# Who makes the second half swap of the rotation: GpSimd in place of ScalarE

## The chip, the cores and the metric

The kernel runs on one core of a Trainium2 chip. A core has five engines that work side by side, each through its own instructions in program order: TensorE (PE, matmuls; PEld is its weight load), VectorE (DVE), ScalarE (ACT), GpSimd (POOL) and SyncE (SP, which here only issues DMAs). They wait for each other through semaphores. The metric is the device time of one execution in microseconds (us), smaller is better.

## What is computed

Two layers of a decoder trunk on 512 tokens of width 1024, in float32. Each layer is a norm, one input projection whose columns feed three token mixers (a state space group, a short convolution group, a sparse attention group), an output projection, and a gated MLP. The change lies in the attention group, where queries and keys are rotated by position:

```python
def apply_rope(x, cos, sin):
    x1, x2 = jnp.split(x, 2, axis=-1)
    ...
    return jnp.concatenate([x1 * c - x2 * s, x2 * c + x1 * s], axis=-1)

q = apply_rope(q.reshape(bsz, s_len, NSA_HEADS, dk), cos, sin) * (dk ** -0.5)
kc = compress_block(rope_k(k_cmp), kpos, kw1, kw2)
...
ks_blocks = rope_k(k_sel).reshape(bsz, n_slc, SEL_BLOCK, dk)
...
kw = jnp.pad(rope_k(k_win), win_pad)
```

A head has 64 channels, so a half is 32. The compressed keys kc and values vc come from a small MLP over blocks of 32 tokens, with a position table added first.

## The kernel before

Activations lie with channels on the 128 partitions and the 512 tokens along the free dimension. A projection tile is 128 output channels: 24 matmuls of 128x512 (`mul3` in `tile_steps`, L260 to L262: eight input blocks, three products of high and low parts) into one PSUM tile `mm`. Each weight tile is loaded by SyncE into `raw` and split into a high part by ScalarE (L227, or L219 for the MLP's weights) and a low part, either by VectorE (L224, L233) or by ScalarE's negated copy (L230, L221) and an accumulating DMA that GpSimd issues (L231, L222). Three `raw` and four `hl` buffers rotate. L262 is the first matmul of three that reads the low part.

Four tiles are rotated in each layer: `cmp` (64 rows rotated, 64 rows of values), `keys`, `q0` and `q1` (128 rows, so two heads of 64). For each, `evac` copies PSUM into a slot `r` (L331, ScalarE), then makes a second slot `sw` with the halves of each head swapped: for every 64 rows one copy of 32 rows up and one of 32 rows down (L333, L334). `rope` (L338 to L340, VectorE) multiplies `r` in place by the cosines, `sw` by the sines, and adds. So there are seven pairs of copies in a layer. The tables `Cr` and `Sr` already hold the norm's factor (L471, L472), which comes through `rstdB` (L316, ScalarE).

After the rope the keys are split into high and low parts on both halves of the partitions (L352, L353 on ScalarE, L354, L355 on VectorE) and the queries too (L396, L397). The rotated `cmp` tile gets its position table added by GpSimd (L373, two adds for each of four parts, with a memset L374 behind), is split (L379 ScalarE, L380 VectorE) and goes into the compress matmuls (L542, eight for each of four parts; their result is copied by L548). The scores are L673 and L676 on TensorE (high and low part of the keys), evacuated by VectorE (L678); probabilities come from ScalarE's exp (L680) and are scaled by VectorE and GpSimd (L687). Then come transposes (L697), their evacuation (L701, L704) and the product with the values (L717). L419 and L420 split the values, L407 to L409 evacuate the projection of small columns.

In which order each engine gets its instructions is set in two steps. The program issues pieces by a table (PLAN: when a piece comes, counted in projection steps). The Tile framework then orders the instructions of all engines by its own planned times and sets the semaphores; an engine afterwards keeps to that order. An edit that makes one instruction look shorter or longer to it, or moves it to another engine, can therefore move others.

Of the kernel before, what the change touches and what calls it, by code (L numbers as in the profile page):

```python
# [12 lines left out]
AF = mybir.ActivationFunctionType  # L13
# [52 lines left out]
def trunk(ctx: ExitStack, tc: tile.TileContext, ins, out):  # L66
    nc = tc.nc
    V, A, G, TE = nc.vector, nc.scalar, nc.gpsimd, nc.tensor
# [7 lines left out]
    def slot(dt=F32, shape=(P, 512)):  # L76
        return ph.tile(list(shape), dt, tag="s", bufs=32, name="s")
# [245 lines left out]
    def mixers(l, norm):  # L323
# [4 lines left out]
        def evac(ps, n):  # L328

            r, sw = slot(), slot()  # L330
            A.activation(r, ps, AF.Copy)  # L331
            for q in range(0, n, 64):
                A.activation(sw[q:q + 32], r[q + 32:q + 64], AF.Copy)  # L333
                A.activation(sw[q + 32:q + 64], r[q:q + 32], AF.Copy)  # L334
            return r, sw

        def rope(r, sw, n):
# [160 lines left out]
        def tile_steps(name, post, rot_n=0):  # L498
            wt = nxt()
            ps = mm()  # L500
            for k in range(KD):
                mul3(ps, wt, k, hs[k][:, 0, :], hs[k][:, 1, :], k == 0, k == KD - 1)
                step()
                if k < KD - 1:
                    yield
            args = evac(ps, rot_n) if rot_n else (ps,)
            if clock[0] < t_spread:
                late.append(lambda: post(*args))
            else:
                post(*args)  # L510
            done[name] = True
            yield
# [470 lines left out]
        r = PLAN["ratio"]  # L983
# [332 lines left out]
```

## Time and profile before

| what | value |
|---|---|
| time of the runs, median of 3 | 1210.34 us (1210.14 to 1210.81) |
| the profiled execution | 1209.18 us, span of the trace 1207.4 us |
| TensorE busy | 1177.0 us, 97% of the span |
| VectorE busy | 931.6 us, 77% |
| ScalarE busy | 664.0 us, 55% |
| GpSimd busy | 170.4 us, 14% |
| the rotated tiles are worked on | about 25 to 62 us (layer 0) and 618 to 652 us (layer 1) |

Busy times are sums over one profiled execution. A row of a time line gives start, duration, engine, line, operation, output and input tile with their shapes and, in square brackets, how long the engine had been idle and what ended that. Matmuls overlap in their rows (a matmul of 128x512 has a row of 0.39 us, and the next one starts 0.23 us later), so distances between starts are read, not durations. Where several instructions of one form follow each other, one row stands for them, with their number behind x.

### The profile page before, as it was taken

Reading aid. Unit: us, or ns where it says so; the run is one execution under the profiler, and the core shown is the slowest. Engines: PE = TensorE matmul, PEld = TensorE weight load, DVE = VectorE, ACT = ScalarE, POOL = GpSimd, SP = SyncE. Lnnn points to the kernel's source line nnn. Section 1 sums busy time; section 2 is a strip of 40 time slices with the busy share of each in tenths; the row PEclk is TensorE's granted clock in tenths of the full one; section 3 lists DMA queues with packets and bytes.
Section 4 is the critical chain, followed back from the end, with each engine's and each line's share of the span. In section 5 each row is a group of like instructions: output and inputs, shape, how many; then the busy total and the mean of one; then the engine's idle time right before and its main releaser. Section 6 shows DMA issues by size and latency. Waiting matters only on the chain.

```text
span 1207.4 us, 17074 instructions
## 1 busy us (share of the span) xinstructions
PE 1177.0 (97%) x6299; PEld 1001.1 (83%) x6299; DVE 931.6 (77%) x1707; ACT 664.0 (55%) x1060; POOL 170.4 (14%) x225
## 2 busy tenths in 40 slices
PE   8899999999999999999998999999999999999997
PEld 7677788888889888988887887888888998889886
DVE  5797879558888778967747887876787968888684
ACT  7885764444544445434569667545444544454464
POOL 2332245100000000000031212640000000000002
PEclk9999999999999999999999999999999999999999
DMA  7774554523225331443255834544232352325332
GB/s 261 180 174 106 122 149 118 153 87 102 91 62 149 122 101 60 129 135 111 81 116 146 189 98 134 158 109 135 88 105 70 106 157 88 105 61 152 119 123 88
DMA packets 46771, 146.07 MB, mean 121 GB/s; under 512 B 5024, under 2 KB 9440, under 8 KB 46688
## 3 DMA queue, kind: packets, MB, share of 16 engines
q1 hardware_dynamic: 36112, 117.71, 29.8%
q0 software_dynamic: 10432, 27.27, 12.7%
q8 instruction: 50, 0.82, 0.3%
q14 instruction: 33, 0.27, 0.1%
q10 hardware_dynamic: 144, 0.00, 0.0%
HBM read 115.57 MB, written 2.13 MB: 97 GB/s over the span
## 4 chain that ended last, share of the span: by engine, by line
PE 70%; DVE 16%; ACT 7%; issue 4%; POOL 1%; DMA 1%; SPq 0%; POOLq 0%; DVEq 0%; ACTq 0%
PE mm L260 16%; PE mm L262 16%; PE mm L261 16%; PE mm L1065 2%; PE mm L1063 2%; PE mm L1064 2%; PE aux L260 2%; PE aux L262 2%; PE aux L261 2%; PE aux L1065 2%; PE aux L1064 2%; PE aux L1063 2%; DVE hl L171 1%; DVE s L1011 1%; PE pv L717 1%
## 5 line engine op out<-in xcount | busy, mean ns | idle before, releaser
L260 PE MATMUL mm<-h,hl 128*128 128x512 f32 x1040 | 410.5, 395 | 0.0
L262 PE MATMUL mm<-h,hl 128*128 128x512 f32 x1040 | 407.3, 392 | 0.9 <-DMA hl<-raw 0.8
L261 PE MATMUL mm<-h,hl 128*128 128x512 f32 x1040 | 407.3, 392 | 0.0
L227 ACT ACTIVATE hl<-raw 128x1024 fp32r<-128x1024 f32 x161 | 170.2, 1057 | 149.1 <-PE mm L262 96.5
L262 PEld LDWEIGHTS mm<-h,hl 128*128 128x128 f32 x1040 | 195.8, 188 | 42.9 <-DMA hl<-raw 1.8
L260 PEld LDWEIGHTS mm<-h,hl 128*128 128x128 f32 x1040 | 195.9, 188 | 39.6 <-issue 0.7
L261 PEld LDWEIGHTS mm<-h,hl 128*128 128x128 f32 x1040 | 196.2, 189 | 38.7 <-issue 0.3
L233 DVE TENSOR_TENSOR hl<-raw,hl 128x1024 fp32r<-128x1024 f32 x119 | 146.2, 1229 | 48.0 <-ACT hl L227 47.2
L1011 DVE SCALAR_TENSOR_TENSOR s<-s,par 128x511 f32<-128x511 f32 (+1 forms) x172 | 128.0, 747 | 11.9 <-ACT s L1009 9.9
L1008 DVE TENSOR_TENSOR s<-mm,rstdB 128x512 f32<-128x512 f32 x86 | 59.0, 688 | 53.1 <-PE mm L262 53.1
L1009 ACT ACTIVATE s<-s,par 128x512 f32<-128x512 f32 x86 | 69.3, 807 | 28.7 <-DVE s L1008 28.1
L169 POOL DMA_DIRECT2D hl<-s x16 | 13.8, 863 | 496.1 <-DVE hl L171 441.7
L319 ACT ACTIVATE s<-s 128x512 fp32r<-128x512 f32 (+2 forms) x78 | 39.6, 524 | 62.5 <-DVE s L1026 57.8
L166 ACT ACTIVATE hl<-s 128x512 fp32r<-128x512 f32 x64 | 38.3, 629 | 54.4 <-PE aux L1065 24.9
L1024 ACT ACTIVATE s<-s 128x512 f32<-128x512 f32 x40 | 25.3, 631 | 57.4 <-DVE s L1011 57.4
L231 POOL DMA_DIRECT2D hl<-raw x42 | 36.5, 869 | 128.1 <-ACT hl L230 81.9
L1065 PE MATMUL mm<-s,hl 128*128 128x256 f32 x192 | 54.3, 283 | 0.0
L1063 PE MATMUL mm<-s,hl 128*128 128x256 f32 x192 | 54.3, 283 | 0.0
L1064 PE MATMUL mm<-s,hl 128*128 128x256 f32 x192 | 54.3, 283 | 0.0
L320 DVE TENSOR_TENSOR s<-s 128x512 fp32r<-128x512 f32 (+2 forms) x78 | 43.9, 578 | 8.9 <-ACT s L319 8.4
L274 POOL TENSOR_TENSOR m<-m,mhalf 128x1 f32<-128x1 f32 (+2 forms) x14 | 10.9, 776 | 259.4 <-DVE m L273 259.4
L230 ACT ACTIVATE hl<-raw 128x1024 fp32r<-128x1024 f32 x42 | 43.9, 1046 | 0.0
(299 smaller groups left out, 2329.9 us busy)
## 6 DMA issues: line engine op xcount, KB each, us to landing
raw<-in_w_up SPq DMA_DIRECT2D x86, 512.0 KB, 3.3
raw<-in_w_dn SPq DMA_DIRECT2D x49, 512.0 KB, 3.3
raw<-in_w_in SPq DMA_DIRECT2D x44, 512.0 KB, 3.7
hl<-raw POOLq DMA_DIRECT2D x44, 512.0 KB, 4.6
raw<-in_w_out SPq DMA_DIRECT2D x16, 512.0 KB, 3.3
raw<-in_w SPq DMA_DIRECT2D x8, 512.0 KB, 4.6
s<-dr SPq DMA_DIRECT2D x16, 256.0 KB, 4.7
hl<-s POOLq DMA_DIRECT2D x16, 256.0 KB, 3.6
```

The costliest lines, as they stand in the source:

```text
L227: A.activation(t[:, 0, 0:w], r[:, 0:w], AF.Copy)
L230: A.activation(t[:, 1, 0:w], r[:, 0:w], AF.Copy, scale=-1.0)
L233: eng.tensor_tensor(t[:, 1, 0:w], r[:, 0:w], t[:, 0, 0:w].bitcast(F32), op=OP.subtract)
L260: TE.matmul(ps, wh, rhs_h, start=first, stop=False)
L261: TE.matmul(ps, wh, rhs_l, start=False, stop=False)
L262: TE.matmul(ps, wl, rhs_h, start=False, stop=last)
L1008: V.tensor_tensor(u, ps, rstdB, op=OP.mult)
L1009: A.activation(acc, u, AF.Identity, scale=w[:, 2:3], bias=pr[:, C_FCB + i:C_FCB + i + 1])
L1011: V.scalar_tensor_tensor(acc[:, j:], u[:, :T - j], w[:, 2 - j:3 - j], acc[:, j:], op0=OP.mult, op1=OP.add)
L1063: TE.matmul(ps, w[:, 0, q], h_, start=first and j == 0, stop=False, skip_group_check=not first)
L1064: TE.matmul(ps, w[:, 0, q], l_, start=False, stop=False, skip_group_check=not first)
L1065: TE.matmul(ps, w[:, 1, q], h_, start=False, stop=j == 3, skip_group_check=not first)
```

## The change

In `evac` the second copy of each pair moves from ScalarE to GpSimd; the first stays.

```diff
             for q in range(0, n, 64):
                 A.activation(sw[q:q + 32], r[q + 32:q + 64], AF.Copy)
-                A.activation(sw[q + 32:q + 64], r[q:q + 32], AF.Copy)
+                G.tensor_copy(sw[q + 32:q + 64], r[q:q + 32])
```

GpSimd gets seven more instructions in each layer, 14 in all, and the order of the other engines changes with it. L338 now waits for GpSimd too, since it overwrites `r`, which the copies read. Four places follow, with the difference of an engine's order, - for before and + for now.

GpSimd, layer 0, from the position adds of the cmp tile on (s<-s,par_87 is a part of that tile with the position table added; the four pairs of L334 are two for keys, two for q0, two for q1):

```order
 L373 TENSOR_TENSOR s<-s,par_87 64x8x31 x4
 L374 MEMSET s 128x8
+L334 COPY s<-s 32x512 x2
 L373 TENSOR_TENSOR s<-s,par_87 64x8x31 x2
 L374 MEMSET s 128x8
 L373 TENSOR_TENSOR s<-s,par_87 64x8x31 x2
 L374 MEMSET s 128x8
-L231 DMA hl<-raw 128x1024 x3
+L334 COPY s<-s 32x512 x2
+L231 DMA hl<-raw 128x1024
+L334 COPY s<-s 32x512 x2
+L231 DMA hl<-raw 128x1024 x2
```

The two copies for the keys stand behind four of the eight adds, those for q0 and q1 behind all of them, and the first DMA L231 of this piece behind q0's copies.

TensorE, layer 0, in the tile behind q1 (h_81 and h_82 are input blocks 2 and 3; aux<-hl,s is the compress matmul):

```order
 L260 MATMUL mm<-h_81,hl 128x512
-L261 MATMUL mm<-h_81,hl 128x512
-L262 MATMUL mm<-h_81,hl 128x512
-L260 MATMUL mm<-h_82,hl 128x512
-L261 MATMUL mm<-h_82,hl 128x512
-L262 MATMUL mm<-h_82,hl 128x512
-L260 MATMUL mm<-h_83,hl 128x512
 L542 MATMUL aux<-hl,s 128x256 x7
 L542 MATMUL aux<-hl,s 64x256
+L261 MATMUL mm<-h_81,hl 128x512
+L262 MATMUL mm<-h_81,hl 128x512
+L260 MATMUL mm<-h_82,hl 128x512
```

The compress matmuls stand six projection matmuls earlier.

GpSimd, layer 1, the same stretch:

```order
 L373 TENSOR_TENSOR s<-s,par_88 64x8x31 x2
 L374 MEMSET s 128x8
-L231 DMA hl<-raw 128x1024 x3
+L231 DMA hl<-raw 128x1024
+L334 COPY s<-s 32x512 x4
+L231 DMA hl<-raw 128x1024
+L334 COPY s<-s 32x512 x2
+L231 DMA hl<-raw 128x1024
```

Here all eight adds and one DMA stand ahead of the copies of keys and q0.

VectorE, layer 1, the rope of the keys (hl<-raw,hl is a weight split):

```order
 L338 TENSOR_TENSOR s<-s,Cr 128x512
 L339 TENSOR_TENSOR s<-s,Sr 128x512
-L224 TENSOR_TENSOR hl<-raw,hl 128x8x128
 L340 TENSOR_TENSOR s<-s 128x512
-L224 TENSOR_TENSOR hl<-raw,hl 128x8x128
+L224 TENSOR_TENSOR hl<-raw,hl 128x8x128 x2
```

The weight split that stood inside the rope stands behind it. On TensorE of layer 1 the first score pairs (L673, L676) move ahead of the last six matmuls of a projection tile, as the compress matmuls do in layer 0. On ScalarE of layer 0 the two L419 move ahead of L316.

## Rows read from the trace of the kernel before

**Rows 1.** TensorE's waits, 20 to 100 us: us in total, times, longest.

```profile
...
PE aux L673 <- DVE s L397: 1.7, 1, 1.7
PE pv L717 <- DVE s L704: 0.5, 1, 0.5
PE mm L262 <- DMA hl<-raw: 0.5, 1, 0.5
```

**Rows 2.** Time line of TensorE, layer 0: start, duration, [idle before <-releaser].

```profile
46.73 1.21 PE L542 MATMUL aux<-hl,s 128*128 128x256 f32 x8 [2.04 <-DVE s L380]
...
48.25 0.60 PE L260 MATMUL mm<-h,hl 128*128 128x512 f32 x1
...
51.63 0.42 PE L262 MATMUL mm<-h,hl 128*128 128x512 f32 x1
...
56.47 0.39 PE L262 MATMUL mm<-h,hl 128*128 128x512 f32 x1
...
61.92 0.45 PE L673 MATMUL aux<-s 128*128 128x512 f32 x1
```

**Rows 3.** Time line of GpSimd, layer 0.

```profile
36.54 4.70 POOL L373 TENSOR_TENSOR s<-s,par 64x248 f32<-64x248 f32 x4 [1.49 <-DVE s L340]
...
51.49 0.86 POOL L231 DMA_DIRECT2D hl<-raw  x1 [6.11 <-DVE s L340]
```

**Rows 4.** Time line of VectorE, layer 0.

```profile
37.00 0.82 DVE L338 TENSOR_TENSOR s<-s,Cr 128x512 f32<-128x512 f32 x1 [0.55 <-ACT s L334]
...
40.57 1.22 DVE L340 TENSOR_TENSOR s<-s 128x512 f32<-128x512 f32 x1
...
46.25 0.76 DVE L380 TENSOR_TENSOR s<-s 128x256 fp32r<-128x256 f32 x2
```

**Rows 5.** Time line of ScalarE, layer 0.

```profile
41.82 0.63 ACT L352 ACTIVATE s<-s 64x512 fp32r<-64x512 f32 x1 [3.77 <-DVE s L340]
...
46.01 0.58 ACT L331 ACTIVATE s<-mm 128x512 f32<-128x512 f32 x1
...
50.16 1.04 ACT L230 ACTIVATE hl<-raw 128x1024 fp32r<-128x1024 f32 x1
```

**Rows 6.** Time line of GpSimd, layer 1.

```profile
623.31 3.42 POOL L373 TENSOR_TENSOR s<-s,par 64x248 f32<-64x248 f32 x4
...
630.84 0.87 POOL L231 DMA_DIRECT2D hl<-raw  x1 [0.41 <-issue]
```

**Rows 7.** Time line of VectorE, layer 1.

```profile
631.40 0.69 DVE L338 TENSOR_TENSOR s<-s,Cr 128x512 f32<-128x512 f32 x1 [3.40 <-ACT s L334]
...
633.74 0.69 DVE L340 TENSOR_TENSOR s<-s 128x512 f32<-128x512 f32 x1
...
638.01 0.76 DVE L380 TENSOR_TENSOR s<-s 128x256 fp32r<-128x256 f32 x2
640.90 0.69 DVE L338 TENSOR_TENSOR s<-s,Cr 128x512 f32<-128x512 f32 x1 [2.12 <-ACT s L334]
```

**Rows 8.** Time line of ScalarE, layer 1.

```profile
634.46 0.63 ACT L352 ACTIVATE s<-s 64x512 fp32r<-64x512 f32 x1 [1.06 <-DVE s L340]
...
637.70 0.58 ACT L331 ACTIVATE s<-mm 128x512 f32<-128x512 f32 x1
...
642.95 1.28 ACT L396 ACTIVATE s<-s 64x512 fp32r<-64x512 f32 x2
```

**Rows 9.** Time line of TensorE, layer 1.

```profile
644.45 0.47 PE L673 MATMUL aux<-s 128*128 128x512 f32 x1 [2.86 <-DVE s L397]
```

**Rows 10.** Prices: line view of L334 (ns min/median/max), then GpSimd's time line.

```profile
L334 ACT ACTIVATE s<-s x14: 625/630/633, 28.3 to 647.9; 32x512 f32<-32x512 f32 x14
...
68.25 1.83 POOL L687 TENSOR_SCALAR s<-s,m 128x512 f32<-128x512 f32 x2 [2.62 <-DVE m L742]
...
100.59 0.52 POOL L708 MEMSET s<- 64x512 f32 x1
```

**Rows 11.** Line view of L231, 20 to 60 us: its three DMAs' time to landing.

```profile
DMA to landing us min/median/max: 4.5/5.1/6.3
```

## Prediction

> **What bounds the kernel now.** The table above has TensorE busy for nearly the whole span, so I first ask where it waits. The view of TensorE's waits for the first mixer stage names, beside 2.0 us before the compress matmuls (L542) [rows 2], 1.7 us before the scores (L673) and two smaller ones behind [rows 1]. The time line of TensorE shows what such a wait costs on top: after the 2.04 us the matmuls start 0.42 us apart from 48.25 to 51.63 (eight intervals), while from 56.47 to 61.92 they run 24 in 5.45 us, 0.227 apart [rows 2]. That is the granted clock at 1.2 instead of 2.4 GHz after an idle stretch; it costs 8 x 0.2 = 1.6 us, with a ninth 1.7. Layer 1 has one such place, 2.86 us before its first scores [rows 9]. Elsewhere TensorE hardly waits, so what the edit does to these two places is what it is worth.
>
> Both places hang on the rotation, which the edit touches. Then I read the other engines there. ScalarE, GpSimd and VectorE each work in program order. In layer 0 the key chain is: copies, rope on VectorE from 37.00 until L340 ends at 40.57 + 1.22 = 41.79 [rows 4], the four key splits L352/L353 on ScalarE from 41.82 [rows 5], then L379, L380 and at 46.73 the compress matmul. While this runs, GpSimd does the position adds L373 (36.54, four in 4.70 us) [rows 3], and VectorE's L340 takes 1.22 us instead of the 0.69 of layer 1 [rows 4, 7]: the two engines slow each other.
>
> **The change, part by part.** *ScalarE loses* 14 copies (L334) of 0.630 us [rows 10], 8.8 us. ScalarE is not the bound; the saving counts only where a consumer waits for it.
>
> *GpSimd gains* 14 copies of 32x512. No row shows this copy. The nearest from below writes as many elements and reads none (MEMSET 64x512, 0.52); from above, L687 reads and writes as many with arithmetic (two in 1.83, so 0.92 each) [rows 10]. I take 0.70, between them: a copy reads too, but computes nothing. The Trainium skill (GPSIMD Engine Reference, section 3.1) gives 769 ns for 512 elements in a tight loop; with 0.77 the sum below would be 0.4 us higher.
>
> *Layer 0, keys.* The order puts the two key copies behind four of the L373, and those wait for the rope of the cmp tile. ScalarE reaches that stretch 0.63 us earlier, but the broadcast L316 now stands behind two L419, which takes it back; so L373 still starts at 36.54. VectorE now has nothing beside it, so I take the four adds at layer 1's 3.42 [rows 6], and 0.1 for the memset: the copies start at 40.1 and end at 41.5. L338 overwrites what the copies read and waits for them: 41.55 instead of 37.00. Queued behind it on VectorE are the whole rope, a weight split L224 and the key splits; on ScalarE, behind L352, also the evacuation of q0. The remaining four L373 run beside the rope as the first four did, so I keep its 4.79 (37.00 to 41.79); alone it took 3.03 in layer 1 (631.40 to 633.74 + 0.69) [rows 7]. L340 ends at 46.35. From L352 to L380 layer 1 took 638.01 - 634.46 = 3.55 [rows 7, 8], and the compress matmul follows 0.48 after L380 (before: 46.25 and 46.73, the L380 in [rows 4]): 50.4 instead of 46.73.
>
> On TensorE the compress matmuls moved ahead of six projection matmuls (6 x 0.227 = 1.36). From their start to the L262 at 56.47, TensorE was busy 9.74 - 1.70 = 8.04 us with the half-speed stretch in it; now 8.04 + 1.36 = 9.40, so it gets there at 59.8 if the scores of q0 don't hold it. They don't: ScalarE needs 46.01 - 41.82 = 4.19 from L352 to q0's evacuation [rows 5], so 50.6; 0.6 for that and 1.4 for the GpSimd copies give L338 at 52.6; from there to the first scores layer 1 took 644.45 - 640.90 = 3.55 [rows 7, 9], so 56.2, and TensorE arrives after 57. The weights of that L262 come with GpSimd's DMA L231: issued at 51.49 before [rows 3], 0.3 after ScalarE's L230 (50.16 + 1.04) [rows 5]; L230 now comes about 3.3 later, so the issue is at 54.75 and the landing, 4.5 to 6.3 later [rows 11], typically at 59.8. Both paths agree: **+3.3 at this point**. Behind it the scalar and vector chains are only some 1.7 late (four copies fewer), so two waits there, 0.5 for L262's weights and 0.5 for L704 [rows 1], can vanish: -1.0. Layer 0: **+2.2**, rounded.
>
> *Layer 1.* There GpSimd's queue has all eight L373 and the DMA L231 (630.84) [rows 6] ahead of the key copies. One copy fewer on ScalarE lets the cmp rope, and so L373, start 0.6 earlier: L231 at 630.2, the copies from 631.05 to 632.45, L338 at 632.5 instead of 631.40 [rows 7]. But the L224 that stood inside the rope now stands behind it, so L340 ends 2.05 later (L338 to L396: 640.90 to 642.95 [rows 7, 8]) at 634.55, as before (634.43). Then q0 gains: L352 to L331 takes 637.70 - 634.46 = 3.24 [rows 8], the evacuation 0.6, two copies 1.4 on GpSimd instead of four on ScalarE: L338 at 639.9 instead of 640.90, and the first scores could start at 643.45, 1.0 earlier. Against this TensorE has moved those scores ahead of six projection matmuls that used to fill the time before the wait: +1.36. Layer 1: **+0.4**.
>
> The other three tiles' copies (cmp in both layers, q1) cost nothing: GpSimd is idle there, and their rope is not the last thing TensorE waits for. If that cover were gone for q1, it would cost the difference of two copies, 1.4 - 1.3 = 0.1.
>
> **Sum**: 2.2 + 0.4 = +2.6. The profiled execution took 1209.18 (span 1207.4 and 1.8 around it), 1.16 below the median of the runs; the sum added to it gives 1211.8, added to the median 1210.34 **1212.9**, which I predict.
>
> **Rivals.** The price of the copy, p, enters six times (two key copies in layer 0, two key and two q0 copies in layer 1), so 0.1 us of p is 0.6 us.
> 1. *The copy is cheap: not slower.* With p = 0.52 the sum is 2.6 - 1.1 = +1.5, 1211.8, no difference that can be told (0.2% is 2.4 us, about what a measurement of this kernel can tell). For it: the memset row. Against: a copy also reads. It decides below p = 0.67. The Trainium skill (GPSIMD Engine Reference, section 4.1) calls one-input operations roughly line rate, an estimate of 512 / 1.2 GHz = 0.43; by that +1.0; no row here shows a one-input copy.
> 2. *The copy is dear and the weights land late.* With p = 0.92 (+1.3) and 6.3 to landing (+1.3): +5.2, 1215.5. For it: L687's row was taken beside VectorE, as q0's copies will be.
> 3. *The relief of ScalarE reaches TensorE: faster.* If layer 0 is absorbed by later waits and layer 1's 2.86 goes: -2.9, 1207.4. For it: ScalarE is full in both stretches. Against it: in layer 0 the order of GpSimd excludes it, and in layer 1 six matmuls less cover the wait.
>
> That the edit isn't carried out is excluded: the order shows 14 copies on GpSimd.
>
> **How the numbers follow.** Forecast case 0.50, of which 0.33 ends above 2.4 us and 0.17 below; rival 1 0.28; rival 2 0.15; rival 3 0.07. Slower 0.33 + 0.15 = 0.48, no difference 0.17 + 0.28 = 0.45, faster 0.07. The range, 1210.4 to 1215.4, leaves out rival 3, the cheapest end of rival 1 and the top of rival 2. Cases of one sign, slower or flat, hold most of it; the forecast's own range is 1212.0 to 1214.0.
>
> **What would show it.** Right: in layer 0 L338 of the keys starts near 41.5 and its idle time is ended by GpSimd's L334; TensorE waits about 6 us before L542, no longer before L673; the copies take 0.6 to 0.8. In layer 1 the first scores start near 643.5 plus layer 0's shift, behind a wait of about 3. Wrong: copies under 0.5 or over 1 us; a rope that runs in 3 us although L373 is beside it (1.8 less in layer 0); a half-speed stretch that falls inside the long wait (1.7 less), or lasts longer after it; or waits after 60 us that grow instead of vanishing, which the moved order in layer 1 could bring.

## The result and the profile after

The changed kernel takes **1216.98 us** (median of 4 runs, 1216.54 to 1218.05); the kernel before took 1210.24 beside it. The ratio is 1.006, 95% interval 1.0047 to 1.0073: **+6.7 us, slower by 0.6%**, where +2.6 was forecast and 1215.4 was the top of the range. The profiled execution took 1218.05 us (span 1216.2, against 1207.4). One run of the kernel before, beside the first four experiments, took 1448.28 us at a granted clock of 0.75 and is left out of what follows.

In layer 0 the two key copies stand where the order had put them, behind four additions. GpSimd's time line, which answers to [rows 3] (start, duration, engine, line):

```profile
36.71 3.14 POOL L373 TENSOR_TENSOR s<-s,par 64x248 f32<-64x248 f32 x4 [0.80 <-DVE s L340]
...
40.08 1.27 POOL L334 COPY s<-s 32x512 f32<-32x512 f32 x2
41.43 2.39 POOL L373 TENSOR_TENSOR s<-s,par 64x248 f32<-64x248 f32 x2
...
50.94 1.76 POOL L334 COPY s<-s 32x512 f32<-32x512 f32 x2 [4.17 <-ACT s L331]
```

VectorE's time line there, as [rows 4]:

```profile
41.38 0.69 DVE L338 TENSOR_TENSOR s<-s,Cr 128x512 f32<-128x512 f32 x1 [4.76 <-POOL s L334]
41.99 1.23 DVE L339 TENSOR_TENSOR s<-s,Sr 128x512 f32<-128x512 f32 x1
...
44.82 1.21 DVE L340 TENSOR_TENSOR s<-s 128x512 f32<-128x512 f32 x1
...
49.19 0.76 DVE L380 TENSOR_TENSOR s<-s 128x256 fp32r<-128x256 f32 x2
```

And TensorE's, as [rows 2]; the L262 at 59.33 is the one that stood at 56.47 before:

```profile
49.67 2.08 PE L542 MATMUL aux<-hl,s 128*128 128x256 f32 x8 [4.50 <-DVE s L380]
...
57.69 0.40 PE L673 MATMUL aux<-s 128*128 128x512 f32 x1
...
59.33 0.40 PE L262 MATMUL mm<-h,hl 128*128 128x512 f32 x1
```

L338 waits for GpSimd's L334, the whole key chain is late with it, and TensorE reaches L262 2.86 us late. The first matmul of layer 1 (L308) then starts 4.65 late (611.87 against 607.22), the span ends 8.8 late. So some 4.2 of the loss in these two executions lies in layer 1, where the prediction had +0.4. TensorE's waits there, 640 to 800 us, name the new thing (us in total, times, longest):

```profile
PE aux L673 <- DVE s L397: 4.4, 2, 4.2
PE aux L611 <- DVE m L605: 1.9, 1, 1.9
```

L611 is the second small product of the compress branch. Before, it ran at 675.93 with no wait. Its operand comes from a chain of tiny steps on VectorE and ScalarE (L601 to L605, with the tanh L604 on ScalarE). ScalarE's time line before:

```profile
671.23 0.24 ACT L604 ACTIVATE m<-m 128x64 f32<-128x64 f32 x1
671.38 0.58 ACT L701 ACTIVATE s<-aux 128x512 fp32r<-128x512 f32 x1
672.90 1.06 ACT L227 ACTIVATE hl<-raw 128x1024 fp32r<-128x1024 f32 x1 [0.94 <-DMA raw<-in_w_in]
```

and after, at the same place of the program:

```profile
674.62 0.59 ACT L701 ACTIVATE s<-aux 128x512 fp32r<-128x512 f32 x1
678.88 1.06 ACT L227 ACTIVATE hl<-raw 128x1024 fp32r<-128x1024 f32 x1 [3.67 <-DMA raw<-in_w_in]
679.84 1.04 ACT L230 ACTIVATE hl<-raw 128x1024 fp32r<-128x1024 f32 x1
680.79 0.61 ACT L436 ACTIVATE s<-s 128x512 f32<-128x512 f32 x1
681.31 0.24 ACT L604 ACTIVATE m<-m 128x64 f32<-128x64 f32 x1
```

The tanh now stands behind a weight split (L227) that waits 3.67 us for its weights to land. It needed nothing but L603, which had run at 676.78. VectorE's L605 stands behind L437, which waits for the same place on ScalarE, and TensorE's L611 stands earlier than it did:

```profile
681.43 0.69 DVE L437 SCALAR_TENSOR_TENSOR s<-s 128x512 f32<-128x512 f32 x1 [3.48 <-ACT s L436]
682.04 0.22 DVE L605 SCALAR_TENSOR_TENSOR m<-m 128x64 f32<-128x64 f32 x1
```

```profile
682.32 0.41 PE L611 MATMUL aux<-m,par 128*128 128x32 f32 x2 [1.91 <-DVE m L605]
...
682.88 0.61 PE L262 MATMUL mm<-h,hl 128*128 128x512 f32 x1
683.29 0.63 PE L260 MATMUL mm<-h,hl 128*128 128x512 f32 x1
683.72 0.63 PE L261 MATMUL mm<-h,hl 128*128 128x512 f32 x1
```

Behind the 1.91 us wait the matmuls run 0.43 apart instead of 0.23, a half-speed stretch that the kernel before does not have there. That ScalarE does not take a ready instruction ahead of a waiting one is what the Trainium skill states too (TensorE: Matmul & The Clock Gate, "Architectural detail: the array is 16× 32×32, not 1× 128×128": its queue is strict first-in-first-out); the rows agree.

### The profile page after: what moved, and what is told of

Its sections match the earlier page's. It is cut to its first block, busy times and chain, and to the rows that moved or that the text cites. A ratio compares the mean times of both kernels' runs of the same rounds, so it can differ in the third digit from the quotient of the medians.

```text
span 1216.2 us, 17096 instructions
## 1 busy us (share of the span) xinstructions
PE 1183.0 (97%) x6299; PEld 1006.9 (83%) x6299; DVE 932.2 (77%) x1707; ACT 655.4 (54%) x1046; POOL 179.9 (15%) x239
## 4 chain that ended last, share of the span: by engine, by line
PE 72%; DVE 15%; ACT 6%; issue 3%; POOL 2%; DMA 2%; SPq 0%; POOLq 0%; DVEq 0%; ACTq 0%
PE mm L260 16%; PE mm L261 16%; PE mm L262 16%; PE mm L1065 2%; PE mm L1063 2%; PE mm L1064 2%; PE aux L260 2%; PE aux L262 2%; PE aux L261 2%; PE aux L1065 2%; PE aux L1064 2%; PE aux L1063 2%; DVE hl L171 1%; PE pv L717 1%; DVE s L1011 1%
## 5 line engine op out<-in xcount | busy, mean ns | idle before, releaser
L262 PE MATMUL mm<-h,hl 128*128 128x512 f32 x1040 | 409.0, 393 | 0.0
L227 ACT ACTIVATE hl<-raw 128x1024 fp32r<-128x1024 f32 x161 | 170.2, 1057 | 155.9 <-PE mm L262 100.1
L262 PEld LDWEIGHTS mm<-h,hl 128*128 128x128 f32 x1040 | 196.9, 189 | 40.6
L231 POOL DMA_DIRECT2D hl<-raw x42 | 36.5, 870 | 110.4 <-ACT hl L230 86.2
```

The lines of the kernel that those rows point to most:

```text
L227: A.activation(t[:, 0, 0:w], r[:, 0:w], AF.Copy)
L262: TE.matmul(ps, wl, rhs_h, start=False, stop=last)
```

## The experiments

All times are medians, each set against runs of the kernel before on the same chip (their medians 1210.24 to 1210.61). "Layer 1's own" is worked out from the one profiled execution of each kernel: how late the span ends against the kernel before, less how late line 308, the first matmul of layer 1, starts.

| kernel | GpSimd's copies in | order of the other queues | time | against before, us | ratio, 95% interval | layer 1's own |
|---|---|---|---|---|---|---|
| after | both layers | moved | 1216.98 | +6.7 | 1.0047 to 1.0073 | +4.2 |
| e1_layer0 | layer 0 | moved in layer 0 | 1212.15 | +1.7 | 1.0004 to 1.0022 | -0.3 |
| e2_layer1 | layer 1 | moved in layer 1 | 1215.52 | +5.1 | 1.0026 to 1.0047 | +4.1 |
| x1_place | both | old | 1211.80 | +1.4 | 0.9999 to 1.0017 | -0.1 |
| x2_order | none | moved | 1214.83 | +4.4 | 1.0023 to 1.0044 | +4.6 |
| f1_tanh | both | moved, tanh in front | 1214.85 | +4.6 | 1.0034 to 1.0060 | +3.3 |
| f2_reverse | none | old, tanh behind | 1210.61 | +0.3 | 0.9997 to 1.0014 | +0.7 |
| f3_layer1_tanh | layer 1 | moved in layer 1, tanh in front | 1213.36 | +3.1 | 1.0014 to 1.0032 | +1.7 |
| g3_helpers | layer 1 | TensorE old, others moved | 1211.38 | +0.8 | 1.0000 to 1.0020 | -0.6 |
| h1_layer1 | layer 1 | as g3, tanh in front | 1209.69 | -0.8 | 0.9990 to 1.0009 | +0.4 |
| f4_early | layer 0, keys early | old | 1208.10 | -2.2 | 0.9972 to 0.9990 | -0.2 |
| g1_both_early | both, keys early | old | 1207.96 | -2.6 | 0.9972 to 0.9991 | +0.1 |
| h2_both | both, keys early | old; layer 1 as h1 | 1208.45 | -2.0 | 0.9975 to 0.9993 | +0.2 |

The last column depends on where an execution ran at half speed. The kernel before does so in layer 1 from 645.6 to 649.0 us, behind the long wait for L673, which costs 1.7 us. The executions of g3_helpers and h2_both have no such stretch there, and that of f1_tanh one twice as long.

### One layer at a time

```diff
-                A.activation(sw[q + 32:q + 64], r[q:q + 32], AF.Copy)
+                G.tensor_copy(sw[q + 32:q + 64], r[q:q + 32]) if l == 0 else A.activation(sw[q + 32:q + 64], r[q:q + 32], AF.Copy)
```

e2_layer1 has `l == 1`. In each, TensorE's order in the layer that is changed is that of the changed kernel, in the other layer that of before.

> The second copies are GpSimd's in layer 0 alone; in layer 0 every queue stands as in the changed kernel, in layer 1 as in the kernel before. The prediction's own sum for this layer is +2.2 us: the keys' copies wait for the four additions of line 373, the scores start 2.9 late (that part was seen in the changed kernel's trace, line 262 at 59.33 against 56.47), and waits further on take 1.0 of it back. The rival, read from the changed kernel's trace: nothing is taken back, a half-speed stretch at 78 to 84 us adds about 1.9, and the layer ends 4.5 us late (line 1063 at 356.1 against 351.6): +4.5. Second rival: the lost clock is a chance of single executions, then +2.9.

> The second copies are GpSimd's in layer 1 alone, with the queues of the changed kernel there and those of the kernel before in layer 0. The prediction's sum for this layer is +0.4 us. The rival, read from the changed kernel's trace: the scores start 0.65 sooner, but line 611 stands six matmuls earlier on TensorE while its operand from line 605 comes later, so a new wait of 1.9 us and a half-speed stretch of about 1.7 behind it: +4 us (+8.8 of the two profiled executions less the 4.65 by which layer 1 began late). If the two layers add up to the +6.7 of the medians, this one gives about 2.2 when layer 0 gives 4.5.

Measured: +1.7 and +5.1, which add up to 6.8. Layer 0 costs what the prediction said, somewhat less; layer 1 costs all that was missing. The wait at L611 is there again with layer 0 untouched. TensorE's longest new wait in e2_layer1, 640 to 800 us, and what ScalarE did ahead of it:

```profile
PE aux L611 <- DVE m L605: 2.3, 1, 2.3
```

```profile
674.11 1.06 ACT L227 ACTIVATE hl<-raw 128x1024 fp32r<-128x1024 f32 x1 [4.02 <-DMA raw<-in_w_in]
...
676.54 0.24 ACT L604 ACTIVATE m<-m 128x64 f32<-128x64 f32 x1
```

Behind that wait TensorE runs at half speed here too. The views by windows give length, busy time and instructions of PE, PEld, DVE, ACT and POOL, then the granted clock, the DMA share and GB/s. First e2_layer1, then the kernel before:

```profile
678.60:682.00 3.40, 3.40 (x9) 2.21 (x7) 3.22 (x9) 2.08 (x6) 1.33 (x2) 0.50 0.97 241
```

```profile
675.00:685.00 10.00, 10.00 (x64) 8.44 (x63) 9.10 (x27) 7.89 (x20) 3.10 (x4) 1.00 0.98 231
```

The two account for nearly all of the profiled execution's loss in layer 1. From L308 to L851, a matmul further on in layer 1, e2_layer1 takes 4.15 us longer than the kernel before. Its listed waits from 640 to 800 us come to 7.9 us against 5.6, 2.3 more, as much as the wait at L611; and 3.4 us at half speed cost 1.7.

### Where the copies run, or the order that came with it

The framework of this kernel sorts each engine's instructions anew at every edit, so the one-line change has two parts. They can be parted: each engine's instructions are tied, one behind the other without a wait, in an order that is written out as a list.

```diff
+    named = {i.name: i for i in nc.cur_bb.bb.instructions}
+    for eng in QUEUES:
+        prev = None
...
+                if prev is not None:
+                    tc.add_manual_dep(named["I-%d" % k], prev, mybir.DependencyInfo(mybir.DependencyClass.NoSync, mybir.DependencyReason.DATA), reason="order")
+                prev = "I-%d" % k
```

x1_place has the changed line and the old lists (GpSimd's: the new one); x2_order has the old line and the new lists.

> The copies are GpSimd's in both layers and GpSimd's queue stands as in the changed kernel, but TensorE, VectorE, ScalarE and the transfers keep, instruction by instruction, the order of the kernel before (less the copies on ScalarE). Theory 'place' (the cost is the wait of the keys' copies behind line 373 and the copies' price): +3 us in layer 0 and about -1 in layer 1, where the scores of the first queries come sooner; with half-speed stretches set off by the longer wait up to +6.7, all of what the change cost. Theory 'order' (the cost is the moved order): the keys are late as before, so still about +2 to +3, but no wait at line 611 and no half-speed stretch at 682 us: +2.2 at most.

> All the copies stay on ScalarE (each second one right behind its first), and every queue keeps, instruction by instruction, the order of the changed kernel. Theory 'order': layer 0 loses 1.4 (the block scores of line 542 stand six matmuls earlier and wait for operands that come no sooner), layer 1 another 1.4 for the six moved matmuls and 1.9 to 3.6 at line 611: +4 to +6.4 us. Theory 'place': at most +1.4, since matmuls moved in front of or behind a wait change only where the wait stands.

Measured: the place alone +1.4, with an interval that just holds no change, the order alone +4.4. The order without a single copy on GpSimd has the wait at L611 (2.4 us) and layer 1's own loss of 4.6. So most of the loss is not what GpSimd does; it is where other instructions came to stand. The place alone costs time in layer 0 (TensorE 2.6 late at line 308) and nothing in layer 1 (2.5 at the end). The two do not add up to the 6.7; what the missing 0.9 is made of was not tested.

### The tanh and the weight split

f1_tanh is the changed kernel with two instructions of layer 1 moved in the lists, L604 on ScalarE and L605 on VectorE; ScalarE's order:

```diff
 L701 ACTIVATE s<-aux 128x512
-L227 ACTIVATE hl<-raw 128x1024
-L230 ACTIVATE hl<-raw 128x1024
-L436 ACTIVATE s<-s 128x512
 L604 ACTIVATE m<-m 128x64
+L227 ACTIVATE hl<-raw 128x1024
+L230 ACTIVATE hl<-raw 128x1024
+L436 ACTIVATE s<-s 128x512
```

f3_layer1_tanh is the same in e2_layer1; f2_reverse moves both the other way in the kernel before.

> The changed kernel with two instructions put elsewhere in layer 1 and every other queue as it was: on ScalarE the tanh of line 604 stands ahead of the weight split of line 227 that waited 3.7 us for its transfer, on VectorE line 605 stands ahead of line 437, which waited 3.5 us for the same split. Theory 'tanh' (TensorE's new wait at line 611 and the half-speed stretch behind it come from those two places alone): 1.9 to 3.6 us of the +6.7 go, so 1213.3 to 1215.0, and down to about 1212 if the 1.3 lost between lines 764 and 851 belongs to it too; no wait at line 611. Theory 'the rest of the order' (the six matmuls that stand elsewhere on TensorE are the cost): line 611 waits still or another wait takes its place, under 1 us of gain.

> The kernel before, all copies on ScalarE, with the reverse of that edit: line 604 stands behind lines 701, 227, 230 and 436 on ScalarE and line 605 behind line 437 on VectorE, as in the changed kernel; TensorE's order is that of before, where line 611 stands some matmuls later. Theory 'tanh' with its slack: line 605 would end at about 676.3 by the trace of before, 0.4 to 0.5 us behind the start of line 611 at 675.93, so a wait of 0.5 and +0.5 us, up to +2 if a half-speed stretch follows it. If the place of the tanh alone made the loss, +3 to +4. If it has no part, 0.

> The kernel with GpSimd's copies in layer 1 alone (+5.1 us), with the same two instructions put back to the front. Theory 'tanh': what is left is the lead of 1.0 us that its trace had at line 596, so 1209.4 to 1210.4, the kernel before or a little faster. Theory 'the rest of the order': 1.9 to 3.6 of the 5.1 go at most, +1.5 to +3.2, and without the wait at line 611 another loss shows.

Measured: 2.2 of the 6.7 and 2.0 of the 5.1 go with the two instructions; both pairs of intervals overlap, so the size of this part is rough. In f1_tanh's time line of ScalarE the tanh runs ahead of the landing, and no wait at L611 is left among TensorE's:

```profile
675.76 0.26 ACT L604 ACTIVATE m<-m 128x64 f32<-128x64 f32 x1 [1.85 <-DVE m L603]
677.57 1.06 ACT L227 ACTIVATE hl<-raw 128x1024 fp32r<-128x1024 f32 x1 [1.55 <-DMA raw<-in_w_in]
```

In the kernel before the late tanh alone costs 0.3, which its interval does not tell from nothing: L611 stands later there, waits 0.3 us, and the rest of the delay is covered. As all queues of f2_reverse are tied, the 0.3 holds the cost of the tying too. The theory that the tanh is all of layer 1's loss falls; 3.1 are left in f3_layer1_tanh.

### TensorE's own moved matmuls

g3_helpers is e2_layer1 with one list exchanged: TensorE's, for that of before. h1_layer1 is that with the tanh in front as well.

```diff
 # g3_helpers: QUEUES of e2_layer1, but
-    "PE": (order of e2_layer1)
+    "PE": (order of the kernel before)
```

> GpSimd's copies in layer 1 alone (+5.1 us with the changed kernel's queues there): TensorE keeps the order of the kernel before, ScalarE, VectorE and GpSimd stand as in the changed kernel, the tanh of line 604 behind the weight split included. Theory 'TensorE's moved matmuls': with line 611 back in its later place the late tanh is hidden but for some 0.5 us (as when the tanh alone was put back in the kernel before: +0.3), and the 3.1 that were left with the tanh in front are gone: 0 to +0.7. Theory 'the helpers' order': the wait at line 611 shrinks by the 1.4 of the six matmuls and the 3.1 stay: +3 to +4.

> GpSimd's copies in layer 1 alone, TensorE in the order of the kernel before, ScalarE, VectorE and GpSimd as in the changed kernel but with the tanh of line 604 and line 605 put to the front: both suspects of layer 1 are undone at once. If TensorE's moved matmuls and the late tanh are all that layer 1 lost, what is left is the lead of the changed kernel there (its scores began 0.65 us sooner): -0.6 or better, 1209.0 to 1210.0. If the helpers' order costs something by itself, the +0.8 that remained with the tanh behind stay: 1211 to 1211.5.

Measured: +0.8 and -0.8; the first has an interval that begins at no change, the second one that holds it. Giving TensorE its old order back takes 4.3 of the 5.1. Yet the wait at L611 is still there in the profiled execution of g3_helpers. Its waits, 640 to 800 us:

```profile
PE aux L673 <- DVE s L397: 2.8, 1, 2.8
PE aux L611 <- DVE m L605: 1.9, 1, 1.9
PE mm L262 <- DMA hl<-raw: 0.9, 1, 0.9
```

and of the kernel before:

```profile
PE aux L673 <- DVE s L397: 2.9, 1, 2.9
PE pv L717 <- DVE s L704: 0.9, 2, 0.5
PE pv L717 <- DVE s L726: 0.6, 2, 0.4
PE aux L673 <- DVE s L704: 0.6, 1, 0.6
PE aux L697 <- POOL s L657: 0.4, 1, 0.4
```

L851 starts at 765.69, earlier than before (766.33), in spite of that wait. But this is the fastest run of g3_helpers (1208.75, the median is 1211.38), and it ran at full speed where the kernel before did not. g3_helpers and the kernel before, by windows:

```profile
645.00:650.00 5.00, 4.99 (x26) 3.94 (x25) 4.45 (x6) 4.12 (x7) 0.37 (x1) 1.00 0.61 143
```

```profile
645.00:650.00 5.00, 5.00 (x20) 4.11 (x19) 2.66 (x5) 4.90 (x8) 0.00 (x0) 0.66 0.69 133
```

So this execution does not show what the wait costs with the old order. h1_layer1 shows it better: it is at half speed there like the kernel before (644.9 to 648.3). Its tanh is in front, and TensorE waits in two other places instead:

```profile
679.39 0.50 PE L717 MATMUL pv<-s 128*128 128x512 f32 x1 [1.44 <-ACT s L701]
684.21 0.28 PE L772 MATMUL aux<-cst,acs 128*32 128x128 f32 x1 [0.87 <-DVE acs L767]
```

With both behind it TensorE is 2.8 us late against the kernel before (L772 stood at 681.40), yet at L851 only 0.5: the smaller waits of the kernel before further on (0.6 at L673, 0.4 at L697, most of the 0.6 for L726) are gone. So in this execution the old order gives most of such a delay back.

f3_layer1_tanh differs from h1_layer1 in TensorE's order alone, and its half-speed stretch is at the same place. To compare the two, one must count the work: in the moved order the first scores and L611 stand six matmuls earlier than in the old one, L764 ten, L851 none. With 0.227 us added for each of them, and the lateness at L308 taken off, f3_layer1_tanh is 0.7 us late at the first scores, 1.0 at L611, 2.5 at L764 and 1.8 at L851; h1_layer1 is 0.6 ahead, level, 1.7 late and 0.5 late. Behind L764 both give back, so most of the 1.3 us between them is lost before L611. The wait before the first scores, which six matmuls no longer shorten, is 3.8 us in f3_layer1_tanh and 2.8 in h1_layer1. By the medians the two kernels differ by 3.9; the rest of that these two executions do not show. What the moved order does to L611 comes on top where the tanh is late. TensorE's moved order with the old order of the other queues was not tried: the two wait for each other.

### The keys' copies ahead of the additions

f4_early has GpSimd's copies in layer 0 alone, all other queues in the old order, and the first additions traced three steps later, so that GpSimd has the keys' copies first. g1_both_early has all fourteen copies on GpSimd with the same early keys and the old order in both layers; h2_both joins the early keys to h1_layer1.

```diff
-                after(PLAN["blk"][i], lambda i=i: add(i // 2, i % 2))
+                after(PLAN["blk"][i] + (3 if l == 0 and i < 2 else 0), lambda i=i: add(i // 2, i % 2))
```

> GpSimd's copies in layer 0 alone, all other queues in the order of the kernel before, but on GpSimd the keys' two copies stand ahead of the eight additions of line 373 and not behind four of them. Theory 'queue' (the loss of layer 0 is the wait behind those additions): the copies end at about 36.6, line 338 starts at 36.7 against 37.0 before, the additions start where they did; 0 to -0.4 us against the kernel before, and the 1.7 of layer 0 are gone. Theory 'price' (the copies slow VectorE and are slowed by it, 0.61 to 1.11 us each): the queries' copies beside VectorE keep half of the loss, +0.9.

> All fourteen second copies are GpSimd's, as in the changed kernel, but the keys' copies of layer 0 stand ahead of the additions of line 373, and TensorE, VectorE, ScalarE and the transfers keep the order of the kernel before in both layers. The place of the copies in layer 1 cost nothing in the kernel with the old order and the copies behind the additions (its trace was 2.6 late at the end of layer 0 and 2.4 at the end of the span). Theory 'queues' (the copies themselves are free, what cost time was where other instructions stood): the -2.2 us of the kernel with early copies in layer 0 alone, 1207.9 to 1208.3, so the same move of work that cost 6.7 gains 2. Theory 'the copies cost in layer 1': 1209 to 1210.

> The fourteen copies on GpSimd, the keys' copies of layer 0 ahead of the additions with the old order of the other queues there, and in layer 1 the queues of the run before this one. If the two layers add, the -2.2 to -2.6 of the early copies and what that run gives: 1207.0 to 1208.0 where it gives -0.6, 1208.5 to 1209 where it gives +0.8.

Measured: -2.2, -2.6 and -2.0; all three intervals lie below 1. g1_both_early does just what the change does, work for work, and is some 9 us faster than the changed kernel and 2.6 faster than the kernel before. GpSimd's and VectorE's time lines of it, layer 0:

```profile
34.10 1.96 POOL L334 COPY s<-s 32x512 f32<-32x512 f32 x2
36.75 2.46 POOL L373 TENSOR_TENSOR s<-s,par 64x248 f32<-64x248 f32 x2 [0.69 <-DVE s L340]
```

```profile
36.53 0.68 DVE L338 TENSOR_TENSOR s<-s,Cr 128x512 f32<-128x512 f32 x1
```

and TensorE's:

```profile
46.66 1.21 PE L542 MATMUL aux<-hl,s 128*128 128x256 f32 x8 [1.77 <-DVE s L380]
...
53.55 0.50 PE L673 MATMUL aux<-s 128*128 128x512 f32 x1 [1.70 <-DVE s L397]
```

The copies run in the time in which GpSimd waited for the rope of the compress tile anyway. L338 starts 0.47 sooner than in [rows 4], the additions only 0.2 later than in [rows 3], and the first scores start 1.6 sooner (55.18 in the kernel before). Line 308 is 1.75 early, the span ends 1.7 early.

The copies do not make these 1.6 us directly. L542 starts only 0.07 sooner, but TensorE then runs at full speed, where the kernel before is at half speed from 48.3 to 51.7 us. The L262 that stands at 51.63 in [rows 2] stands at 50.03 here, and ScalarE's L219, which waits for it, comes 1.6 sooner, and behind it the queries' splits and the scores. The kernel before, then g1_both_early:

```profile
52.09 1.06 ACT L219 ACTIVATE hl<-raw 128x1024 fp32r<-128x1024 f32 x1 [0.90 <-PE mm L262]
```

```profile
50.45 1.06 ACT L219 ACTIVATE hl<-raw 128x1024 fp32r<-128x1024 f32 x1 [0.53 <-PE mm L262]
```

That three kernels with early keys are faster in the median of 11 runs each is shown. Why they spend less time at half speed is not.

## Why the prediction came out as it did

**What it said of layer 0 held, in part by luck.** Copies from 40.08 to 41.35 (said: 40.1 to 41.5), L338 at 41.38 (41.55), L340's end at 46.03 (46.35), L542 at 49.67 (50.4), L231 issued at 54.44 (54.75), L262 late by 2.86 (3.3), no wait before L673. Two things came otherwise. The wait before L542 was 4.50 us, not about 6: this execution ran at half speed from 24.1 to 27.5 us as well, which the kernel before did not, and TensorE came to the wait 1.8 us later. And the half-speed stretch behind the wait lasted until 54.8, 5.1 us from the start of L542, where the kernel before has 3.4; the prediction had named that as a sign of being wrong. L542's earlier start hid it at L262.

Alone, layer 0 costs 1.7 by the medians. The prediction's own terms, 3.3 less 1.0, give 2.3, where it wrote 2.2. The size is near, but of the two waits that were to make up the 1.0 only L262's 0.5 went. In the changed kernel the one for L704 stays at 0.55, and two new ones of 0.24 and 0.30 stand at L697. There 78.7 to 82.1 us also ran at half speed, and it is 4.4 us late at line 1063 (355.7 against 351.3).

**The price of the copy was set too high, and mattered little.** The lines of L334 after:

```profile
L334 POOL COPY s<-s x14: 601/610/1112, 27.2 to 649.6; 32x512 f32<-32x512 f32 x14
...
  DVE s L338: 12.2, 4
```

0.61 us is the median, 0.60 the least, where 0.70 was taken; the last line says that VectorE's L338 waited 12.2 us for these copies, in four places; before, it waited 11.8 us for ScalarE's L334, in seven. Two copies beside VectorE's L224 took 1.76. The Trainium skill (GPSIMD Engine Reference, section 3.1) gives 0.77 for 512 elements in a tight loop, above the 0.61 of this copy. The Trainium skill (GPSIMD Engine Reference, section 4.1) calls one-input operations roughly line rate; the estimate of 0.43 worked out from it is below the least copy here, 0.60. Rival 1, which rested on a cheap copy, had the copy right and the outcome wrong.

**The first half of layer 1 held too.** With layer 0's 4.65 added, the key copies were due at 635.70 and came at 635.81, L338 at 637.15 and came at 637.10, the queries' L338 at 644.55 and came at 644.93, the first scores at 648.10 and came at 648.46. The wait before them was 4.18 us, where about 3 was said.

**The step that failed is the last term of layer 1**: "Against this TensorE has moved those scores ahead of six projection matmuls that used to fill the time before the wait: +1.36. Layer 1: **+0.4**". The sum stopped at the first scores and counted a moved matmul as its own 0.227 us. The order had moved further on as well: the tanh behind a split that waits for a transfer, L605 behind L437, L611 six matmuls sooner. Alone, layer 1 cost 5.1 us by the medians where it was given 0.4. At the first scores the term was near: they start 0.64 sooner in e2_layer1, with 1.36 of work moved behind them, +0.7. Behind them come the wait at L611 (2.3) and the half-speed stretch that follows it (1.7), two terms that the sum did not have; that execution lost 4.15 in the layer up to L851. It could have been seen. The order of the changed kernel has L604 behind L227, and the trace of before showed that this L227 waited 0.94 us for its transfer already. The prediction named "waits after 60 us that grow instead of vanishing, which the moved order in layer 1 could bring" as what would make it wrong, and gave it no price.

**The rivals.** Rival 2 (dear copies, late landing, +5.2) would have come nearest to the size, for a wrong reason: the copies were cheap. Rival 3 (ScalarE's relief reaches TensorE, -2.9) was excluded rightly for this order, "in layer 0 the order of GpSimd excludes it". With the order mended its size comes, -2.6 in g1_both_early, but not by its way: layer 1's wait before the scores stays (3.5 us there), and f4_early, with GpSimd's copies in layer 0 alone, has -2.2 already.

## What to carry over

Where a scheduler sorts the queues anew at every edit, a one-line move of work is two changes: the work, and the order of everything else. Compare the order to the end of the layer, not to the first place that the edit touches, and look above all for a small instruction of a long chain that has come to stand behind one that waits for a transfer. Test the two apart by holding the order fixed. Here the same move of work took 2.6 us off with the keys' copies early and all other queues in their old order, and the new order by itself cost 4.4.

## What the runs showed of the hardware

GpSimd's copy of 32x512 floats has no one price. In the changed kernel it took 0.60 to 1.11 us, median 0.61. In g1_both_early, the fastest kernel, where more of the copies fall beside VectorE's work, the line view has a median of 0.71 and 1.51 at most:

```profile
L334 POOL COPY s<-s x14: 601/708/1514, 27.1 to 643.9; 32x512 f32<-32x512 f32 x14
```

VectorE pays as well: in the changed kernel L339 took 1.23 us beside GpSimd's additions in layer 0 and 0.68 in layer 1 with GpSimd idle. That the dearer copies stand in the faster kernel shows how little their price counted.

TensorE's half-speed stretches do not belong to a program alone. The changed kernel and e1_layer0 have the same layer 0, and from 71 to 78.5 us TensorE's time lines show the same waits (0.24 to 0.30 us at L697, 0.55 at L717) within 0.03 us. Yet the granted clock differs. The changed kernel by windows:

```profile
80.00:82.00 2.00, 2.00 (x6) 1.51 (x6) 1.75 (x10) 0.00 (x0) 0.86 (x1) 0.50 0.61 109
```

and e1_layer0:

```profile
80.00:82.00 2.00, 2.00 (x11) 1.75 (x10) 1.56 (x10) 1.60 (x2) 0.76 (x1) 1.00 0.46 74
```

Of four profiled executions with this order of layer 0, two (the changed kernel, x2_order) fell to 1.2 GHz here and two (e1_layer0, f1_tanh) stayed at 2.4. The Trainium skill (TensorE: Matmul & The Clock Gate, Part 1) says that the point at which the clock rises varies from run to run. In these four executions more varied than that: whether the clock fell at all. What tips it here was not tested.

Half-speed stretches also make most of the spread of e2_layer1's runs, and a large part of the difference between some kernels. In e2_layer1 the two shortest runs (1212.46 and 1213.19 us) had a mean granted clock of 0.993, the two longest (1217.82 and 1218.36) 0.988; 0.005 of such a run is 6.1 us, and the spread is 5.9. The mean over the runs is 0.9932 for the kernel before (beside the first four experiments), 0.9904 for e2_layer1, 0.9895 for the changed kernel and 0.9948 for g1_both_early. One minus the clock, times the span, is an estimate of the time lost at half speed: 8.2, 11.7, 12.8 and 6.3 us. By it about 3.5 of the 5.1 us of e2_layer1, 4.5 of the changed kernel's 6.7, and 1.9 of the 2.6 that g1_both_early gains are clock. It is an upper estimate, since the half speed at the end of every run is in it, where TensorE has little left to do (0.43 us in the last 7.3 of the kernel before). So by this estimate the order cost more in half speed than in the waits themselves. In the profiled execution of e2_layer1, its second shortest run, half speed is 1.7 of 4.15. Which stretches the longer runs had is not known, since only one run of each kernel was profiled.
